# An overflow branch moved ahead of the last down block, splits held behind the norm, and the kernel's end in smaller parts

## The chip, the cores and the metric

The kernel runs on one core of a Trainium2 chip. The metric is the device time of one execution in microseconds, the median over runs of the same program. The core has five engines with queues of their own: TensorE (PE; its weight loads are listed as PEld), VectorE (DVE), ScalarE (ACT), GpSimd (POOL) and SyncE (SP), which only issues transfers here.

## The reference

Two blocks run one after the other on 256 tokens of width 1024. The first has two layers; each is a mixer (gated linear attention beside a gated spatial unit), a cross attention to 256 memory rows and a mixture of 16 experts, each followed by a layer norm. The second has one layer: a mixer (block attention beside a state-space scan), a mixture of 16 experts, and a gated addition before a last RMS norm. The parts that the change touches:

```
def grouped_moe(x, w_router, b_router, w_gate, w_up, w_down):
    ...
    for e in range(N_EXPERTS):
        h = jax.nn.silu(xt @ w_gate[e]) * (xt @ w_up[e])
        y = y + gate[:, e:e + 1] * (h @ w_down[e])
...
    x = layer_norm(DN_ALPHA * x + h, ln_g[l, 2], ln_b[l, 2])
...
# second_block, after hier_moe
    x = x + jax.nn.sigmoid(x @ w_ple_gate[i]) * (p[i] @ w_ple_proj[i])
return rms_norm(x, final_norm_g)
```

Each token uses two of the 16 experts. `hier_moe` in the second block computes the same sum over experts with another router.

## The kernel before

**Dense projections.** A float32 weight is loaded as pieces of up to 1 MB into `raw` buffers (`load`, line 156) and split into a high and a low part (`piece`, line 166, which calls `split`, line 221): ScalarE copies the high part to `whl`, VectorE subtracts it from the weight (lines 98 and 78 of the profile). Three matmuls make one product: high by high, high by low, low by high. There are six `whl` buffers of 2 x 512 columns.

**Experts.** `moe` (line 848) gathers up to 64 tokens for each expert and goes over the experts in eight pairs. For each pair come two up blocks (`up`, two times 16 matmuls a half), a product of both (`middle`), flips of it (`turned`), and the down block of the pair before (`down`, line 981). The evictions of a down block are a scaled copy on ScalarE (`dh` or, in the last pair, `dd`) and a scaled difference on VectorE (`dl`, `dd`), and `spread` (line 1002) brings them back to the tokens, adding into four PSUM tiles `Y` (`ysum`). The last pair has its down block and two spreads behind the loop. Expert weights are 96 transfers of 1 MB in a fixed order on SyncE's queue, into whatever buffers come free (`raw`, `whl`'s, `t8`'s and `vec`'s).

**Overflow.** Each expert has 64 places. If one was chosen by more tokens, a flag is set (line 1025), and `overflow` (line 1036) adds what is missing to `Y` in a loop over the experts, under a branch on every engine (flag load at line 1042, branch at line 1043). With these inputs the flag is not set. The branch is coded behind the last spread and behind `fill("next")`, which issues the loads of the next layer's first weights.

**What follows an expert layer.** In the first block `layer_norm` (line 280): residual sums of `x` with `Y`, mean and variance (in the second layer with a square on ScalarE), normalising, and `turn` (line 445), which flips `x` on TensorE (`trp`), applies gain and offset per column on ScalarE and VectorE alternately (`t`) and splits it (`xTh`, `xTl`). The products of `x` itself with gain and offset are put off to `flush` (line 502), which the next mixer calls behind its second projection in the first block and behind its first in the second block. Behind the first layer the value projection of the memory (`mem_v`, `acc<-whl,mTh`) is coded ahead of the norm. In the second block `tail` (line 1376) adds `Y`, turns `x`, projects it, and ends with the gated sum, the norm over 1024 columns (`rms_norm`, line 466) and one store per half of the tokens (line 1406).

**What sets the order.** A planner orders the instructions of each engine ahead of time by a simulated timeline and moves work over the branch where nothing forbids it. Instructions inside `urgent(name)` are preferred if the name is in `hp`; `after(ins)` queues what is traced inside it behind `ins` on that engine; matmuls of the expert layer and all loads on SyncE keep their written order.

Of the kernel before, what the change touches and what calls it, by code (L numbers as in the profile page):

```python
# [11 lines left out]
OP = mybir.AluOpType  # L12
# [11 lines left out]

class Net:
    def __init__(self, tc, aps, cap=CAP, fallback=True, layers=2, bufs=(7, 6, 9, 2), flex=(1, 2, 2), late=2,
                 hp=("ln", "xm"), ao=1, plat=7, an=((0, 4), (0, 5), 0)):
        self.hp = hp
        self.ao = ao
        self.plat = plat  # L30
        self.an = an
        self.late = late
        self.flex = flex
        self.early = {}
        self.ready = {}
        self.due = []
        self.bufs = bufs
        self.layers = layers
        self.tc, self.nc, self.a = tc, tc.nc, aps
        self.cap = cap  # L40
        self.fallback = fallback
# [124 lines left out]
    def piece(self, W, k0, segs, nk=4):  # L166

        key = W.tensor.name, W.offset, k0, segs[0][0]
        if key in self.ready:
            return self.ready.pop(key)  # L170
        raw = self.early.pop(key, None)
        if raw is None:
            raw = self.load(W, k0, segs, nk)
        n = raw.shape[-1]
        gr = self.GR if n <= 512 else 1
        out = []
        for j in range(0, nk, gr):
            hl = self.sb.tile([128, 2, gr, n], F32R, tag="hl", name="whl", bufs=self.NHL)
            self.split(hl[:, 0], hl[:, 1], raw[:, j:j + gr])
            out += [(hl[:, 0, i], hl[:, 1, i]) for i in range(gr)]  # L180
        return out

# [94 lines left out]
            self.nc.gpsimd.dma_start(v[:, i, :n], self.bcast(a, n))  # L277
        return v

    def layer_norm(self, x, l, i, at_once=False):  # L280


        nc = self.nc
        v = self.vec([self.a["ln_g"][l, i], self.a["ln_b"][l, i]])
        r = self.t8("xTh", [128, KT, T], F32R), self.t8("xTl", [128, KT, T], F32R)
        gb = self.cols[:, 0, i], self.cols[:, 1, i]

        tmp = {}

        def part(tt, c, A):  # L290
            with self.urgent("ln"):
                return steps(tt, c, A)

        def steps(tt, c, A):
            o = [x[:, tt, i * 512:(i + 1) * 512] for i in range(2)]
            if c == 0:
                tmp[tt] = self.sm("st", [128, 2, 6])
            st = tmp[tt]
            with self.after(tmp.get("first")):
                if at_once:  # L300
                    self.stt(o[c], o[c], ALPHA, A, OP.mult, OP.add, accum_out=st[:, 0, c:c + 1])
                else:
                    self.stt(o[c], o[c], ALPHA, A, OP.mult, OP.add)
                    nc.vector.bn_stats(st[:, c, :], o[c])
            if c == 0:
                return
            mv = self.sm("mv", [128, 2])
            rs = self.sm("rs", [128, 1])
            if at_once:
                self.ts(mv[:, 0:1], st[:, 0, 0:1], st[:, 0, 1:2], -1.0 / D, OP.add, OP.mult)  # L310
                tmp["first"] = self.ts(mv[:, 1:2], mv[:, 0:1], 0.03125, None, OP.mult).ins
                ss = self.sm("ss", [128, 1])
                self.act(r[1][:, :, tt * 128:(tt + 1) * 128], x[:, tt, :].rearrange("p (a b) -> p a b", a=KT), AF.Square,
                         scale=0.03125, bias=mv[:, 1:2], accum_out=ss)
                self.rsqrt(rs, ss, 1e-5, near=True)
            else:
                nc.vector.bn_aggr(mv, st)
                self.rsqrt(rs, mv[:, 1:2], 1e-5, near=True)
            for c in range(2):
                self.ts(o[c], o[c], mv[:, 0:1], rs, OP.add if at_once else OP.subtract, OP.mult)  # L320
                self.turn(r, x, tt, c, gb)

            def rest():
                self.mul(x[:, tt, :], x[:, tt, :], v[:, 0, :])
                self.add(x[:, tt, :], x[:, tt, :], v[:, 1, :])
            self.due.append(rest)
        return part, r
# [117 lines left out]
    def turn(self, r, x, tt, c, gb=None):  # L445

        p = self.rp([128, 4, 128], "trp")
        for j in range(4):
            kk = 4 * c + j
            last = self.nc.tensor.transpose(p[:, j, :], x[:, tt, kk * 128:(kk + 1) * 128], self.ident)  # L450
        o = [t[:, 4 * c:4 * c + 4, tt * 128:(tt + 1) * 128] for t in r]
        if gb:
            t = self.s2("t32", [128, 4, 128])
            for j in range(4):
                g, b = (v[:, 4 * c + j:4 * c + j + 1] for v in gb)
                if j % 2:
                    self.ts(t[:, j, :], p[:, j, :], g, b, OP.mult, OP.add)
                else:
                    self.act(t[:, j, :], p[:, j, :], AF.Identity, scale=g, bias=b)
            self.anchor = self.split(o[0], o[1], t).ins  # L460
        elif len(o) == 2:
            self.split(o[0], o[1], p)
        else:
            return last.ins, self.cp(o[0], p).ins
# [36 lines left out]

    def flush(self):

        for f in self.due:
            with self.tc.issue_after(self.anchor):
                f()
        self.due = []
# [340 lines left out]
    def moe(self, lg, xs, second, finish, gc, route, Wg, Wu, Wd, fill, source):  # L848
# [129 lines left out]
                    h = slice(64 * s, 64 * s + 64)  # L978
                    self.ts(DT[i][h], p[h, s], self.slot[h], None, OP.is_equal)

        def down(i, apart=False):

            h = H.pop(i)
            ps = [self.rp([128, 512], "dn") for _ in range(2)]
            ws = {(s, jh): self.expert(W, 2, 2 * i + s, jh) for jh in range(2) for s in range(2)}
            todo = [(f, c) for c in range(2) for f in range(4)] if apart else \
                [(f, c) for f in range(4) for c in range(2)]
            for f, c in todo:
                for s in range(2):
                    self.mmp(ps[c][64 * s:64 * s + 64], h[:, f, 64 * s:64 * s + 64],  # L990
                             ws[s, f // 2][:, f % 2, c * 512:(c + 1) * 512], f == 0, f == 3)
            PS[i] = []
            with self.urgent("dn"):
                room = self.t8("dd", [128, 2, 2, 512], F32R) if apart else None
                for c, p in enumerate(ps):
                    dh, dl = (room[:, c, 0], room[:, c, 1]) if apart else \
                        (self.s2(n, [128, 512], F32R) for n in ("dh", "dl"))
                    self.act(dh, p, AF.Copy, scale=gsl[:, i:i + 1])
                    self.stt(dl, p, gsl[:, i:i + 1], dh.bitcast(F32), OP.mult, OP.subtract)
                    PS[i].append((dh, dl))  # L1000
# [10 lines left out]
        for i in range(NE // 2):  # L1011
            pg = up(i, 0)
            if i > 1:
                spread(i - 2)
            gather(i // 2 * 4 + 4, (4 * (i % 2),))
            pu = up(i, 1)
            h = middle(pg, pu)
            if i:
                down(i - 1)
            gather(i // 2 * 4 + 4, (4 * (i % 2) + 2,))  # L1020
            if i == 0:
                slot_gates()
            if i == last and over:
                self.tc.keep_in_program_order(
                    nc.vector.tensor_scalar(flag, cm, float(self.cap), None, op0=OP.is_gt))
            rows(i)
            fill(i)
            turned(i, h)
        down(last, True)
        spread(last - 1)  # L1030
        spread(last)
        fill("next")
        self.overflow(over, Y, source, Wg, Wu, Wd)
        return Y

    def overflow(self, over, Y, source, Wg, Wu, Wd):
# [339 lines left out]
    def tail(self, x, Y, ple):  # L1376
# [3 lines left out]
        for tt in range(2):  # L1380
            for c in range(2):
                o = x[:, tt, c * 512:(c + 1) * 512]
                self.add(o, o, Y[tt, c])
                self.turn(xT, x, tt, c)
        out = self.t8("fin")

        def part(tt, c, A):
            g = self.s2("pg8", [128, 512])
            s = slice(c * 512, (c + 1) * 512)
            self.act(g, A, AF.Sigmoid)  # L1390
            self.mul(ple[:, tt, s], ple[:, tt, s], g)
            self.add(ple[:, tt, s], ple[:, tt, s], x[:, tt, s])
            if c:
                self.rms_norm(ple, None, out, v, (tt,))
        self.proj_full(xT, a["w_ple_gate_2"][0], part)
        return out

    def run(self, out, upto=None):
        tc = self.tc
        self.NRAW, self.NHL, self.NT8, self.GR = self.bufs  # L1400
        with tc.tile_pool(name="sb", bufs=1) as self.sb, \
                tc.tile_pool(name="ps", bufs=1, space=PSUM) as self.ps:
            r = self.body(upto)
            o = out[0].rearrange("(t p) d -> p t d", p=128)
            for tt in range(2):
                self.nc.sync.dma_start(o[:, tt, :], r[:, tt, :])

    def body(self, upto):
        nc, a = self.nc, self.a
# [7 lines left out]
        for l in range(self.layers):  # L1417
# [59 lines left out]
                    vs(0)  # L1477
            Y = self.moe(*got, gc, self.route1, a["w_gate"][l], a["w_up"][l], a["w_down"][l], fill, x)
            fill("tail")
            part, xT = self.layer_norm(x, l, 2, l + self.ao > 1)  # L1480
            for tt in range(2):
                for c in range(2):
                    part(tt, c, Y[tt, c])
# [60 lines left out]
```

## Time and profile before

| what | value |
|---|---|
| median of 3 runs | 1460.03 us (1458.52 to 3515.89) |
| profiled execution, own time | 1460.11 us |
| its span | 1458.3 us |
| mean granted clock of TensorE | 0.976 |
| TensorE matmuls busy | 94% of the span |
| VectorE, ScalarE busy | 44%, 35% |
| bytes read | 419.18 MB |

The span goes from the first to the last instruction. Busy shares are means over stages of different kinds: the three expert layers lie near 265 to 485, 705 to 926 and 1200 to 1420 us; the rest are projections, attention and scans. In a timeline row the columns are start, duration (of all merged instructions), engine, line, operation, output and inputs, shapes, count, and in brackets the idle time before and what ended it.

### The profile page before, as it was taken

How to read it: one execution, taken by the hardware profiler on the slowest of the kernel's cores; microseconds unless marked ns; L12 is line 12 of the kernel's file. 1: busy time of each engine (PE TensorE's matmuls, PEld its weight loads, DVE VectorE, ACT ScalarE, POOL GpSimd, SP SyncE). 2: the span in 40 equal slices, each digit the busy share in tenths (PEclk: the TensorE clock that was granted, in tenths of full speed). 3: DMA queues.
4: the chain of work that ended last, by engine and by line, in shares of the span. 5: the costliest groups of instructions: out<-in, count | busy, mean ns of one | idle time of the engine just before them, and what ended most of it. 6: DMA issues, size and time to landing. Idle time of an engine off the chain costs nothing. (4 is left out here: it accounts for less than half of the span.)

```text
span 1458.3 us, 18050 instructions
## 1 busy us (share of the span) xinstructions
PE 1375.7 (94%) x7258; PEld 899.7 (62%) x7258; DVE 636.3 (44%) x1088; ACT 504.8 (35%) x784; POOL 63.7 (4%) x107
## 2 busy tenths in 40 slices
PE   8999999999988898999899998799999979999987
PEld 7889897444433686898444433499878864444335
DVE  5754754412111767654512111657776641212134
ACT  5634443211101474443211101548764440111132
POOL 2110000000000103000000000000000000000000
PEclk9999999999999999999899999899999989999998
DMA  9745557799999965446799999844534679999991
GB/s 341 271 173 173 174 178 267 280 399 421 420 419 420 320 224 175 145 174 243 297 404 380 422 420 420 326 133 134 185 129 137 227 288 378 421 380 420 420 380 44
DMA packets 101964, 421.50 MB, mean 289 GB/s; under 512 B 10676, under 2 KB 10896, under 8 KB 65008
## 3 DMA queue, kind: packets, MB, share of 16 engines
q1 hardware_dynamic: 97968, 409.17, 72.4%
q0 software_dynamic: 3904, 11.09, 2.3%
q8 instruction: 60, 0.98, 0.3%
q14 instruction: 32, 0.26, 0.0%
HBM read 419.18 MB, written 1.05 MB: 288 GB/s over the span
## 5 line engine op out<-in xcount | busy, mean ns | idle before, releaser
L64 PE MATMUL gu<-we,XG 128*64 128x512 f32 x1536 | 347.0, 596 | 4.2 <-DMA we<-in_w_up_dram 1.9
L78 DVE TENSOR_TENSOR whl<-raw,whl 128x1024 fp32r<-128x1024 f32 (+1 forms) x210 | 241.1, 1163 | 144.6 <-ACT whl L98 143.7
L98 ACT ACTIVATE whl<-raw 128x1024 fp32r<-128x1024 f32 (+1 forms) x210 | 208.2, 1009 | 200.8 <-PE acc L64 97.2
L64 PEld LDWEIGHTS gu<-we,XG 128*64 128x64 f32 x1536 | 108.1, 137 | 208.2 <-issue 193.9
L64 PE MATMUL acc<-whl,xTh 128*128 128x512 f32 (+2 forms) x640 | 193.0, 387 | 4.6 <-ACT xTh L98 3.4
L64 PE MATMUL dn<-we,mid 128*64 128x512 f32 x768 | 179.3, 599 | 16.0 <-DMA we<-in_w_down_dram 13.9
L64 PEld LDWEIGHTS dn<-we,mid 128*64 128x64 f32 x768 | 58.0, 138 | 130.2 <-issue 101.6
L64 PEld LDWEIGHTS acc<-whl,xTh 128*128 128x128 f32 x640 | 119.6, 194 | 29.9 <-ACT xTh L98 4.0
L64 PE MATMUL facc<-xTh,whl 128*128 128x256 f32 x640 | 123.8, 289 | 1.7 <-ACT xTh L98 1.7
L64 PE MATMUL acc<-whl,xTl 128*128 128x512 f32 (+1 forms) x320 | 119.8, 385 | 0.2 <-DVE xTl L78 0.2
L95 ACT ACTIVATE dh<-dn,gsl 128x512 fp32r<-128x512 f32 x42 | 28.9, 688 | 258.8 <-PE dn L64 258.8
L78 DVE TENSOR_TENSOR mid<-mid,gu 128x512 f32<-128x512 f32 x24 | 25.3, 1056 | 211.3 <-PE gu L64 138.7
L64 PEld LDWEIGHTS facc<-xTh,whl 128*128 128x128 f32 x640 | 103.2, 195 | 2.4 <-ACT xTh L98 1.9
L64 PE MATMUL facc<-xTl,whl 128*128 128x256 f32 x320 | 91.6, 287 | 0.0
L87 DVE SCALAR_TENSOR_TENSOR dl<-dn,gsl,dh 128x512 fp32r<-128x512 f32 x42 | 31.5, 750 | 127.6 <-ACT dh L95 125.2
L95 ACT ACTIVATE XG<-gath,gc 128x256 f32<-128x256 f32 x48 | 25.3, 535 | 125.8 <-PE gath L64 117.8
L64 PEld LDWEIGHTS acc<-whl,xTl 128*128 128x128 f32 x320 | 60.5, 193 | 12.7 <-issue 0.7
L64 PEld LDWEIGHTS facc<-xTl,whl 128*128 128x128 f32 x320 | 61.9, 193 | 0.5 <-issue 0.3
L92 DVE TENSOR_SCALAR XG<-gath,gc 128x256 f32<-128x256 f32 x32 | 17.1, 543 | 100.6 <-ACT XG L95 100.2
L95 ACT ACTIVATE mid<-gu 128x512 f32<-128x512 f32 x24 | 14.3, 595 | 121.9 <-PE gu L64 115.4
L64 PE MATMUL acc<-whl,oTh 128*128 128x512 f32 x160 | 49.5, 402 | 0.5 <-ACT oTh L98 0.5
L64 PEld LDWEIGHTS gath<-Dm,xsh 128*128 128x128 f32 x192 | 30.7, 221 | 27.0 <-issue 17.1
(366 smaller groups left out, 1759.3 us busy)
## 6 DMA issues: line engine op xcount, KB each, us to landing
we<-in_w_gate_dram SPq DMA_DIRECT2D x96, 1024.0 KB, 12.7
we<-in_w_up_dram SPq DMA_DIRECT2D x96, 1024.0 KB, 11.8
we<-in_w_down_dram SPq DMA_DIRECT2D x96, 1024.0 KB, 16.7
raw<-in_w_in_dram SPq DMA_DIRECT2D x38, 1024.0 KB, 10.2
raw<-in_w_out_dram SPq DMA_DIRECT2D x12, 1024.0 KB, 5.0
raw<-in_wk_x_dram SPq DMA_DIRECT2D x8, 1024.0 KB, 9.1
raw<-in_wv_x_dram SPq DMA_DIRECT2D x8, 1024.0 KB, 5.7
raw<-in_wq_x_dram SPq DMA_DIRECT2D x8, 1024.0 KB, 5.0
```

The source lines that it names most:

```text
L64: return self.nc.tensor.matmul(out, lhsT=l, rhs=r, start=start, stop=stop, skip_group_check=True)
L78: return self.nc.vector.tensor_tensor(out, a, b, op=op)
L87: return self.nc.vector.scalar_tensor_tensor(out, a, s, b, op0=op0, op1=op1, **k)
L92: return self.nc.vector.tensor_scalar(out, a, s1, s2, op0=op0, op1=op1)
L95: return self.nc.scalar.activation(out, a, f, **k)
L98: return self.nc.scalar.activation(out, a, AF.Copy)
```

## The change

- `overflow` is called behind the eight pairs but ahead of the last down block. The last pair's down weights are requested ahead of it and handed to `down`; the flag is set one pair earlier. `fill("next")` stays behind the spreads and so comes behind the branch.
- `layer_norm` remembers, where `hold` is given (the last norm of each layer of the first block), the last normalising instruction on VectorE and ScalarE's last affine instruction in the turn of the last half of the tokens; until `flush`, splits of weights are queued behind these two.
- `"dn"` joins `hp`, so the evictions of all down blocks are preferred.
- In `tail` the sums of squares are taken per piece as it is made (512 columns, and two times 256 for the second half of the columns), the mean's scaling step moves from GpSimd to VectorE, and the final product and the stores are done in halves of 512 columns.

```diff
-                 hp=("ln", "xm"), ao=1, plat=7, an=((0, 4), (0, 5), 0)):
+                 hp=("ln", "xm", "dn"), ao=1, plat=7, an=((0, 4), (0, 5), 0)):
...
-            self.split(hl[:, 0], hl[:, 1], raw[:, j:j + gr])
+            with self.after(self.hold and self.hold[0]), self.after(self.hold and self.hold[1]):
+                self.split(hl[:, 0], hl[:, 1], raw[:, j:j + gr])
...
-                self.ts(o[c], o[c], mv[:, 0:1], rs, OP.add if at_once else OP.subtract, OP.mult)
-                self.turn(r, x, tt, c, gb)
+                n = self.ts(o[c], o[c], mv[:, 0:1], rs, OP.add if at_once else OP.subtract, OP.mult)
+                a = self.turn(r, x, tt, c, gb)
+            if tt and hold:
+                self.hold = n.ins, a
...
-                    self.act(t[:, j, :], p[:, j, :], AF.Identity, scale=g, bias=b)
+                    first = self.act(t[:, j, :], p[:, j, :], AF.Identity, scale=g, bias=b)
             self.anchor = self.split(o[0], o[1], t).ins
+            return first.ins
...
     def flush(self):
+        self.hold = None
...
-        def down(i, apart=False):
+        def down(i, apart=False, held=None):
...
-            ws = {(s, jh): self.expert(W, 2, 2 * i + s, jh) for jh in range(2) for s in range(2)}
+            ws = held or {(s, jh): self.expert(W, 2, 2 * i + s, jh) for jh in range(2) for s in range(2)}
...
-            if i == last and over:
+            if i == last - 1 and over:
...
-        down(last, True)
+        held = {(s, jh): self.expert(W, 2, 2 * last + s, jh) for jh in range(2) for s in range(2)}
+        self.overflow(over, Y, source, Wg, Wu, Wd)
+        down(last, True, held)
         spread(last - 1)
         spread(last)
         fill("next")
-        self.overflow(over, Y, source, Wg, Wu, Wd)
...
         def part(tt, c, A):
+            if c == 0:
+                ss[tt] = self.sm("ss4", [128, 4])
             g = self.s2("pg8", [128, 512])
-            s = slice(c * 512, (c + 1) * 512)
-            self.act(g, A, AF.Sigmoid)
-            self.mul(ple[:, tt, s], ple[:, tt, s], g)
-            self.add(ple[:, tt, s], ple[:, tt, s], x[:, tt, s])
+            for i, (c0, n) in enumerate(((0, 256), (256, 256)) if c else ((0, 512),)):
+                s, w = slice(c * 512 + c0, c * 512 + c0 + n), slice(c0, c0 + n)
+                self.act(g[:, w], A[:, w], AF.Sigmoid)
+                self.mul(ple[:, tt, s], ple[:, tt, s], g[:, w])
+                self.add(ple[:, tt, s], ple[:, tt, s], x[:, tt, s])
+                self.act(out[:, tt, s], ple[:, tt, s], AF.Square, scale=0.03125, accum_out=ss[tt][:, c + i:c + i + 1])
             if c:
-                self.rms_norm(ple, None, out, v, (tt,))
+                rs = self.sm("rs", [128, 1])
+                self.stt(rs, ss[tt][:, 0:1], ss[tt][:, 1:2], ss[tt][:, 2:3], OP.add, OP.add)
+                self.rsqrt(rs, rs, 1e-6, near=True)
+                for h in range(2):
+                    s = slice(h * 512, h * 512 + 512)
+                    self.stt(out[:, tt, s], ple[:, tt, s], rs, v[:, 0, s], OP.mult, OP.mult)
+                    self.nc.sync.dma_start(o[:, tt, s], out[:, tt, s])
...
-            part, xT = self.layer_norm(x, l, 2, l + self.ao > 1)
+            part, xT = self.layer_norm(x, l, 2, l + self.ao > 1, True)
```

## Rows read from the trace of the kernel before

**Rows 1.** The page: busy time of engines; costliest groups (busy, mean ns, idle before).

```profile
PE 1375.7 (94%) x7258; PEld 899.7 (62%) x7258; DVE 636.3 (44%) x1088; ACT 504.8 (35%) x784; POOL 63.7 (4%) x107
...
L95 ACT ACTIVATE dh<-dn,gsl 128x512 fp32r<-128x512 f32 x42 | 28.9, 688 | 258.8 <-PE dn L64 258.8
```

**Rows 2.** Timeline of PE, first junction (columns as told above).

```profile
486.81 0.73 PE L64 MATMUL acc<-whl,mTh 128*128 128x512 f32 x2 [0.87 <-DVE x L87]
...
502.81 0.39 PE L64 MATMUL acc<-whl,xTh 128*128 128x272 f32 x1 [2.79 <-ACT xTh L98]
```

**Rows 3.** Timeline of PE, second junction.

```profile
926.17 0.96 PE L64 MATMUL ysum<-dd,DT 128*128 128x512 f32 x3 [1.04 <-DVE dd L87]
933.06 3.67 PE L450 MATMUL trp<-ident,x 128*128 128x128 f32 x16 [5.92 <-DVE x L92]
937.35 1.22 PE L64 MATMUL acc<-whl,xTh 128*128 128x512 f32 x2 [0.62 <-ACT xTh L98]
```

**Rows 4.** Timeline of PE, third junction.

```profile
1420.25 0.96 PE L64 MATMUL ysum<-dd,DT 128*128 128x512 f32 x3 [0.91 <-DVE dd L87]
...
1426.60 1.64 PE L64 MATMUL acc<-whl,xTh 128*128 128x512 f32 x6
```

**Rows 5.** Stretches: length, busy (x instructions) of each engine, PEclk, DMA share, GB/s.

```profile
505.00:508.00 3.00, 3.00 (x15) 3.00 (x15) 3.00 (x4) 0.00 (x0) 0.00 (x0) 0.50 1.05 388
927.20:933.00 5.80, 0.00 (x0) 0.00 (x0) 5.04 (x17) 2.28 (x3) 0.56 (x1) 0.57 1.05 388
933.00:941.50 8.50, 7.82 (x26) 6.38 (x27) 7.41 (x17) 5.62 (x14) 0.55 (x1) 0.50 0.76 281
```

**Rows 6.** Timeline of ACT, second and third junction.

```profile
922.00 2.01 ACT L98 ACTIVATE whl<-raw 128x1024 fp32r<-128x1024 f32 x2 [0.76 <-PE dn L64]
923.91 0.67 ACT L95 ACTIVATE dd<-dn,gsl 128x512 fp32r<-128x512 f32 x1
...
1416.09 2.01 ACT L98 ACTIVATE whl<-raw 128x1024 fp32r<-128x1024 f32 x2 [0.73 <-DMA raw<-in_w_ple_gate_dram]
1418.00 0.67 ACT L95 ACTIVATE dd<-dn,gsl 128x512 fp32r<-128x512 f32 x1
```

**Rows 7.** Timeline of DVE, first and second junction.

```profile
505.20 4.62 DVE L78 TENSOR_TENSOR x<-x,vec 128x1024 f32<-128x1024 f32 x4
...
927.40 0.69 DVE L87 SCALAR_TENSOR_TENSOR x<-x,ysum 128x512 f32<-128x512 f32 x1 [0.15 <-DVEq L1043]
...
928.62 1.22 DVE L78 TENSOR_TENSOR whl<-raw,whl 128x1024 fp32r<-128x1024 f32 x1
```

**Rows 8.** Timelines of ACT and DVE at the end; the stores' landing.

```profile
1448.81 0.60 ACT L95 ACTIVATE pg<-acc 128x512 f32<-128x512 f32 x1 [1.75 <-PE acc L64]
1451.02 1.06 ACT L95 ACTIVATE fin<-ple 128x1024 f32<-128x1024 f32 x1 [1.62 <-DVE ple L78]
...
1453.11 1.28 DVE L87 SCALAR_TENSOR_TENSOR fin<-ple,rs,vec 128x1024 f32<-128x1024 f32 x1 [2.20 <-POOL rs L104]
...
DMA to landing us min/median/max: 2.6/2.6/2.6
```

**Rows 9.** Lines 1042, 1043: xcount, duration ns min/median/max, first and last start.

```profile
L1042 PEldq TENSOR_LOAD <-flag x3: 306/312/501, 483.6 to 1420.3; - x3
...
L1043 ACTq COMPARE_BRANCH  x3: 45/45/50, 482.8 to 1419.2; - x3
...
L1043 PEldq COMPARE_BRANCH  x3: 323/330/450, 484.3 to 1420.7; - x3
```

**Rows 10.** Timeline of PE at the first junction, last down block.

```profile
474.82 1.51 PE L64 MATMUL dn<-we,mid 128*64 128x512 f32 x6 [0.69 <-ACT mid L98]
```

**Rows 11.** SP: waits (total us, times, longest), third junction; a load at 496.

```profile
SPq L1043 <- SPq L1043: 14.1, 1, 14.1
...
L161 SPq DMA_DIRECT2D raw<-in_w_in_dram x1: 368/368/368, 496.1 to 496.1; - x1
...
DMA to landing us min/median/max: 5.2/5.2/5.2
```

More of the change, by code (lines that the diff above doesn't have):

```diff
@@ L278, in vec, with layer_norm @@
         return v
-    def layer_norm(self, x, l, i, at_once=False):
+    def layer_norm(self, x, l, i, at_once=False, hold=False):
         nc = self.nc
@@ L502, in flush @@
     def flush(self):
+        self.hold = None
         for f in self.due:
@@ L1385, in tail @@
         out = self.t8("fin")
+        o = self.out[0].rearrange("(t p) d -> p t d", p=128)
+        ss = {}
         def part(tt, c, A):
+            if c == 0:
+                ss[tt] = self.sm("ss4", [128, 4])
             g = self.s2("pg8", [128, 512])
-            s = slice(c * 512, (c + 1) * 512)
-            self.act(g, A, AF.Sigmoid)
-            self.mul(ple[:, tt, s], ple[:, tt, s], g)
-            self.add(ple[:, tt, s], ple[:, tt, s], x[:, tt, s])
-            if c:
-                self.rms_norm(ple, None, out, v, (tt,))
+            for i, (c0, n) in enumerate(((0, 256), (256, 256)) if c else ((0, 512),)):
[4 more added lines that the diff above has]
+                self.act(out[:, tt, s], ple[:, tt, s], AF.Square, scale=0.03125, accum_out=ss[tt][:, c + i:c + i + 1])
+            if c:
+                rs = self.sm("rs", [128, 1])
[5 more added lines that the diff above has]
+                    self.nc.sync.dma_start(o[:, tt, s], out[:, tt, s])
         self.proj_full(xT, a["w_ple_gate_2"][0], part)
@@ L1402, in run @@
                 tc.tile_pool(name="ps", bufs=1, space=PSUM) as self.ps:
[L1403 to L1406, printed above, removed]
+            self.out = out
+            self.body(upto)
     def body(self, upto):
```

## The prediction

> **What bounds the kernel now.** I read the page first, then the granted clock by stretch, then the timelines of single engines at the three places that the edits touch, and last the branch itself. TensorE is busy for 1375.7 us of the span [rows 1], so all its waiting is 82.6 us, and an edit that moves evictions, splits and a branch can give back only the part that lies at its own places: the three ends of an expert layer (near 485, 926 and 1420 us; I call them junctions) and the kernel's end. The reader is to see at each junction what TensorE waits for. At the first it waits 0.87 us behind the spread, then fills the norm with the next layer's value projection, and waits 2.79 us for the turned x [rows 2]. At the second there is nothing to fill with: it waits 1.04 us for the last eviction, 5.92 us for the norm and 0.62 us for the turned x [rows 3]. At the third it waits 0.91 us for the last eviction, and dense projection work starts only at 1426.60 [rows 4]. Around the first two the granted clock falls to 0.50, the lower level of 1.2 GHz: for 3.0 us at the first, and for nearly all of 8.5 us at the second, 7.8 of them busy, behind a stretch with no matmul at all [rows 5].
>
> Second reading: what stands in front of the late operation. At the second junction ScalarE runs two splits of the next weights (2.01 us) right before it evicts the last half of the down block at 923.91; at the third the same, 2.01 us before 1418.00 [rows 6]. VectorE puts a 1.22 us split between the pieces of the residual sum, 0.69 us each [rows 7]. So each part of the change has something to remove, but little of it.
>
> **The change part by part.** The sum stands against the profiled execution's own 1460.11 us (span 1458.3, the rest around it), which is the median of the runs shown (1460.03) but for 0.08.
>
> First junction (branch earlier, splits held, eviction first). What can go: 0.87 + 2.79 us of waiting, and half of the 3.0 us at clock 0.50, which is 1.5; together 5.2. What stays: the turn of x, its affine part on ScalarE and VectorE and its split must still follow the flips, unless the flips get in among the projection's matmuls. I take the first wait whole (0.9, x is read while the spread still runs), half of the second (1.4), half of the clock's part (0.7): 3.0. Bounds: 5.2, and below nothing, since the held splits move onto the path (under the rivals).
>
> Second junction. Eviction first: 1.0 gained. The residual sum of the first column no longer waits for a branch behind the spread: two pieces can lie beside the spread, about 0.6 us apart, 1.2, and the 1.22 us split leaves the norm's chain: 2.4 off the 5.92 us wait. Against it: the weights' first split, so far done ahead of the norm's end [rows 7], now follows the last normalised piece, one ScalarE split of 1.0 us and one VectorE split of 1.22, and is late next: −2.2. Of the four held splits only the first is on the path; the others run beside matmuls on the one before. I keep the clock's loss as it is (half of the 7.8 us, 3.9), since TensorE still idles through the norm. Sum 1.2. Bounds: −2.2, and 1.0 + 2.4 + half of 3.9, 5.3.
>
> Third junction (nothing is held there: the hold ends at the flush before). Eviction first 0.9, two pieces of x beside the spread 1.2: I take 2.1. Bounds: 4.1 (the 0.91 and half of the 6.35 us from 1420.25 to 1426.60, since flips and the split of x stay), and −1.3 (second rival).
>
> The kernel's end. After the last matmul the chain is sigmoid, two VectorE operations, a square over 1024 columns of 1.06 us, two GpSimd steps, a product of 1.28 us, and a store that lands 2.6 us after its issue [rows 8]. With halves, the first half's sigmoid, product and sum run beside the second's on the other engine, and the last square covers 256 columns: I count 0.5. The first GpSimd step becomes a short VectorE one (0.1), the product's second half replaces the whole (half of 1.28 is hidden behind the first store's issue, but the second still follows: 0.2), and the store is half as big: 0.4 of its 2.6. Sum 1.2; bounds 0 (shorter operations mostly pay their fixed part) and 2.5 (square, product and store all halved: 0.53 + 0.64 + 1.3). The added squares and issues for the earlier pieces lie beside TensorE's last matmuls.
>
> The branch before the last down block. On TensorE's sequencer it is a flag load of 0.31, a compare of 0.32 to 0.45 and one event [rows 9]. There TensorE already waits 0.69 us for the turned hidden units [rows 10], and sequencer work can run beside queued flips, so I charge 0.3 us at each of three branches, 0.9; bounds 0 and the whole 0.31 + 0.45 each, 2.3. The compare on ScalarE takes 0.05 [rows 9], and the rows show no engine standing still behind this branch with its inputs ready. The Trainium skill, "Runtime: NRT & Kernel Launch", section "Instruction fetch mechanics", speaks against this: a taken branch to a page that is not loaded stops the engine until the page has come. By that rule the upper bound of this term would hold and the time be 1454.9; by the rows it is 1453.5.
>
> Everything else at zero. The 42 evictions that gain priority already start when the matmuls end: ScalarE's wait before them is 258.8 us, all put down to TensorE [rows 1], and the expert loop is fed by weights in order. The flag is one small VectorE operation moved one pair earlier, beside the loop. SyncE's issue order up to the last down weights is the same.
>
> SyncE itself is the step whose price the trace hides. Behind its branch it executes eight event waits; at the third junction these take 14.1 us, until every transfer issued before has landed [rows 11]. Now this costs nothing, because the next weights are issued ahead of it. If they come behind it, the first goes out when the last down weights have landed, into an empty queue, where 1 MB takes 5.2 us from its issue [rows 11], in place of the 2.7 that 1.05 MB takes in a full one at 388 GB/s [rows 5]: 2.5 us late at each junction. At the second the held splits come later than that; at the first the first projection has the spread ahead of it. I take zero, as work coded behind the branch is already seen ahead of it (the splits at 1416.09 are coded behind it, and ScalarE's branch is at 1419.2 [rows 6, 9]); the price is in the second rival.
>
> Sum: 3.0 + 1.2 + 2.1 + 1.2 − 0.9 = 6.6, and 1460.1 − 6.6 = 1453.5.
>
> **The rivals.** First, slower: the hold only moves the wait. If the norm's chain gets no shorter, the first projection waits for splits that used to be ready. Its place is the first matmul on the new x at the first two junctions. Price: at the second 2.2; at the first half of that for 528 columns in place of 1024, 1.1, and, if the four operations on x (4.62 us) come between the norm and the low halves, 4.6 more [rows 7]. It decides when the part of these 7.9 us that comes exceeds what the rest gives (1.0 + 2.1 + 1.2 − 0.9 = 3.4); all of it makes 1460.1 + 7.9 − 3.4 = 1464.6. For it: VectorE has no free moment in the 3 us after the first new matmuls [rows 5]. Against: those operations are coded behind the first projection's splits.
>
> Second: SyncE's event waits stand in front of the next weights. ScalarE's order at the third junction puts a split of the second piece before the last eviction [rows 6]; weights 2.5 us later move that eviction from 1418.00 to 1420.5: its 0.9 becomes −2.5, and the 2.1 becomes −1.3. Time: 1453.5 + 3.4 = 1456.9.
>
> Third: the change does not do what it says. The compiler already carries work across the branch, so its place may not matter; then the overlap of x with the spread and the shorter norm are not new, and the two evictions and the end are left: 1.0 + 0.9 + 1.2 = 3.1, 1457.0.
>
> Fourth: everything fits and all bounds are reached, 5.2 + 5.3 + 4.1 + 2.5 = 17.1: 1443.0.
>
> **How the numbers follow.** Forecast (1450 to 1456.5) 0.45; first rival 0.18; second 0.12; third 0.13; fourth, from 1450 down, 0.12. The range 1445 to 1465 takes in the second and third rival and most of the first, and leaves out the far end of the fourth and the first rival's worst. A measurement of this kernel can tell about 2% (29 us) from no change; only a reshuffled schedule far from the junctions reaches that: faster 0.02, within 0.95, slower 0.03.
>
> **What would show it.** Right: no split of next weights between the last two evictions at 922; TensorE's wait before the flips of the second junction near 3.5 us instead of 5.92, with a new wait of 1 to 2 us for the first split; dense work of the third junction 2 us sooner after its last down matmul; from the last sigmoid's start to the end of the span 8.3 instead of 9.5 us [rows 8]. Wrong: a wait on the first split above 4 us at the first junction; next weights that land 2.5 us later and an eviction behind them; a gap of 1 us on TensorE between the hidden units' flips and the last down block.

## The result, and the profile after

The changed kernel takes 1467.65 us in the median of 9 runs (1466.09 to 1472.97), the kernel before 1460.88 in the 9 runs beside it (1456.47 to 1464.54, and one far off at 3515.89 that the ratio leaves out): ratio 1.0052, 95% interval 1.0038 to 1.0066, slower by half a per cent. The profiled execution took 1466.9 us, 6.8 more than before's, with a span of 1465.1 us.

I cut both traces into four stretches by landmarks on TensorE: **A** from the first matmul of the first layer's last down block to the first `po` (an output product) of the mixer behind it; **B** the same for the second layer; **C** from the third layer's first `plp` matmul (the product with `w_ple_proj`) to the first matmul of the last two spreads; **D** from there to the end of the span. First the landmarks of the kernel before that were not shown yet (A begins with [rows 10]), as rows of its PE timeline, then those of after with TensorE's waits:

```profile
566.61 0.62 PE L64 MATMUL po<-S,qT 128*64 128x256 f32 x2 [0.79 <-DVE S L611]
...
911.90 0.65 PE L64 MATMUL dn<-we,mid 128*64 128x512 f32 x2 [0.69 <-ACT mid L98]
...
988.40 0.77 PE L64 MATMUL po<-va,apT 128*128 128x64 f32 x5
...
1402.03 1.18 PE L64 MATMUL plp<-whl,pT 128*128 128x512 f32 x4
...
1416.07 0.50 PE L64 MATMUL ysum<-dh,DT 128*128 128x512 f32 x1
```

```profile
472.67 7.09 PE L65 MATMUL dn<-we,mid 128*64 128x512 f32 x32 [0.82 <-ACTq L1050]
484.61 0.73 PE L65 MATMUL acc<-whl,mTh 128*128 128x512 f32 x2 [0.76 <-DVE x L88]
...
501.19 0.59 PE L65 MATMUL acc<-whl,xTh 128*128 128x272 f32 x1 [3.37 <-ACT whl L99]
...
565.43 0.62 PE L65 MATMUL po<-S,qT 128*64 128x256 f32 x2 [0.79 <-DVE S L617]
...
911.85 0.65 PE L65 MATMUL dn<-we,mid 128*64 128x512 f32 x2 [0.73 <-ACTq L1050]
...
923.65 2.00 PE L65 MATMUL ysum<-dd,DT 128*128 128x512 f32 x8
929.18 3.81 PE L454 MATMUL trp<-ident,x 128*128 128x128 f32 x16 [3.52 <-DVE x L93]
936.01 0.80 PE L65 MATMUL acc<-whl,xTh 128*128 128x512 f32 x1 [3.02 <-ACT whl L99]
937.27 0.80 PE L65 MATMUL acc<-whl,xTh 128*128 128x512 f32 x1 [0.47 <-DVE whl L79]
...
988.06 0.88 PE L65 MATMUL po<-va,apT 128*128 128x64 f32 x6
...
1401.65 2.81 PE L65 MATMUL plp<-whl,pT 128*128 128x512 f32 x11
...
1413.67 1.94 PE L65 MATMUL dn<-we,mid 128*64 128x512 f32 x2 [5.73 <-DMA we<-in_w_down_dram]
1416.55 4.34 PE L65 MATMUL dn<-we,mid 128*64 128x512 f32 x8 [0.94 <-DMA we<-in_w_down_dram]
1422.27 5.36 PE L65 MATMUL dn<-we,mid 128*64 128x512 f32 x22 [1.38 <-SPq L1050]
1427.57 0.50 PE L65 MATMUL ysum<-dh,DT 128*128 128x512 f32 x1
```

The reader is to see two things. The first two junctions hardly moved: the wait for the flips at the second is 3.52 us in place of 5.92 [rows 3], but behind it stands a new one, 3.02 and 0.47 us for the first split of the weights. And in the third layer the last down block now waits for its own weights, 5.73 + 0.94 + 1.38 us (the last is put down to SyncE's branch, which has no work for TensorE; at that moment the last down weight lands); before it waited 0.74 us in all. The page says the same in one group: idle time before the down matmuls is 23.2 us, 20.2 of it for the DMA; before it was 16.0 and 13.9. SyncE's timeline says why, after first and then before:

```profile
1387.05 12.40 SPq L162 DMA_DIRECT2D raw<-in_w_ple_gate_dram  x4
1399.50 4.32 SPq L215 DMA_DIRECT2D we<-in_w_down_dram  x4
```

```profile
1385.56 16.50 SPq L213 DMA_DIRECT2D we<-in_w_down_dram  x4
1402.10 4.38 SPq L161 DMA_DIRECT2D raw<-in_w_ple_gate_dram  x4
```

The next weights (`w_ple_gate`, four transfers of 1 MB) have overtaken the last four down weights. These go out from 1399.50 to 1403.4 and land 14.0 to 18.8 us later, the last at 1422.2; in the kernel before the last down weight lands at 1410.6. Of C's 11.9 us more, 7.3 are waits; the rest is that the same matmuls take longer, ten of them at a mean granted clock of 0.66 between 1413.6 and 1422.2 us. What sets the end of C is the last landing: the last 22 matmuls start with it, at 1422.27. The PE rows above answer to [rows 2 to 4] and [rows 10]; those that answer to the other groups follow, one fence a view and with its columns: the page [rows 1], a stretch [rows 5], ScalarE [rows 6 and 8], VectorE [rows 7], the stores' landing [rows 8], the branch [rows 9] and SyncE's wait at the third junction [rows 11]:

```profile
PE 1379.8 (94%) x7258; PEld 898.7 (61%) x7258; DVE 637.0 (43%) x1098; ACT 504.4 (34%) x794; POOL 62.0 (4%) x105
...
L65 PE MATMUL dn<-we,mid 128*64 128x512 f32 x768 | 183.8, 604 | 23.2 <-DMA we<-in_w_down_dram 20.2
```

```profile
933.00:941.50 8.50, 5.03 (x11) 3.66 (x12) 8.14 (x12) 8.50 (x13) 0.00 (x0) 0.50 0.31 94
```

```profile
921.81 0.69 ACT L96 ACTIVATE dd<-dn,gsl 128x512 fp32r<-128x512 f32 x1 [2.75 <-PE dn L65]
...
934.89 5.79 ACT L99 ACTIVATE whl<-raw 128x1024 fp32r<-128x1024 f32 x6
940.57 1.16 ACT L99 ACTIVATE xTh<-t 128x512 fp32r<-128x512 f32 x2
...
1456.85 0.66 ACT L96 ACTIVATE pg<-acc 128x256 f32<-128x256 f32 x2 [2.20 <-PE acc L65]
```

```profile
924.32 0.69 DVE L88 SCALAR_TENSOR_TENSOR x<-x,ysum 128x512 f32<-128x512 f32 x1 [1.03 <-PE ysum L65]
```

```profile
DMA to landing us min/median/max: 2.0/2.0/2.1
```

```profile
L1050 PEldq COMPARE_BRANCH  x3: 318/318/353, 471.8 to 1405.5; - x3
L1050 ACTq COMPARE_BRANCH  x3: 45/45/50, 472.4 to 1408.3; - x3
```

```profile
SPq L1050 <- SPq L1050: 18.3, 1, 18.3
```

ScalarE evicts the second junction's last half at 921.81 in place of 923.91, idle for 2.75 us before it, and the residual sum starts at 924.32 in place of 927.40; but then it runs the six held splits in a row, 5.79 us, with half of x's high parts behind them. The end takes 1465.1 − 1456.85 = 8.3 us, and a half store lands in 2.0 us in place of 2.6.

All kernels of the study by the four stretches (us, from the landmark rows of each trace; the kernels are told below):

| kernel | A | B | C | D |
|---|---|---|---|---|
| before | 91.8 | 76.5 | 14.0 | 42.2 |
| after | 92.8 | 76.2 | 25.9 | 37.6 |
| e1 after, loads in order | 91.6 | 76.4 | 14.3 | 40.8 |
| e2 before, branch moved | 90.2 | 76.3 | 25.9 | 38.7 |
| e3 after, no hold | 90.5 | 76.1 | 26.0 | 37.6 |
| e4 before, hold | 92.7 | 78.1 | 14.0 | 42.4 |
| e5 before, four weights ahead | 91.3 | 76.6 | 24.8 | 39.6 |
| e6 before, two ahead | 91.3 | 76.6 | 21.1 | 39.6 |
| e7 e1, two splits free | 90.1 | 73.0 | 14.4 | 40.3 |
| e8 e1, no hold | 90.6 | 76.2 | 14.2 | 40.9 |
| e9 before, new end | 91.7 | 76.4 | 14.0 | 41.2 |
| e10 e7, branch at the old place | 91.1 | 74.3 | 14.3 | 41.0 |
| e11 e7, three free | 89.8 | 73.0 | 14.4 | 40.3 |
| e12 e7, no priority | 90.0 | 73.0 | 14.4 | 40.3 |

Before, e5, e6 and e9 have the same work in A and B: 91.3 to 91.8 and 76.4 to 76.6 is how well a stretch repeats. After and e1 differ in A by 1.2 with the same work, so A is good to about 1 us. One cause is in after's ScalarE timeline: two splits ahead of the last eviction at the first junction wait for a value weight, which e1's do not:

```profile
478.71 2.01 ACT L99 ACTIVATE whl<-raw 128x1024 fp32r<-128x1024 f32 x2 [1.66 <-DMA raw<-in_wv_x_dram]
```

After against before: +1.0, −0.3, +11.9, −4.6, in all +8.0; the span differs by 6.8. The rest lies outside the stretches: A begins 2.2 us earlier in that one execution, which e1 (1.5 us later there) doesn't repeat, and from A's end to B's start it takes 1.1 us longer.

### The profile page after: what moved, and what is told of

Same layout as the page of the kernel before. It is cut to its first block, busy times and chain, and to the rows that moved or that the text cites. A ratio compares the mean times of both kernels' runs of the same rounds, so it can differ in the third digit from the quotient of the medians.

```text
span 1465.1 us, 18082 instructions
## 1 busy us (share of the span) xinstructions
PE 1379.8 (94%) x7258; PEld 898.7 (61%) x7258; DVE 637.0 (43%) x1098; ACT 504.4 (34%) x794; POOL 62.0 (4%) x105
## 5 line engine op out<-in xcount | busy, mean ns | idle before, releaser
L65 PE MATMUL dn<-we,mid 128*64 128x512 f32 x768 | 183.8, 604 | 23.2 <-DMA we<-in_w_down_dram 20.2
L65 PEld LDWEIGHTS acc<-whl,xTl 128*128 128x128 f32 x320 | 60.7, 193 | 11.9 <-issue 0.3
L96 ACT ACTIVATE mid<-gu 128x512 f32<-128x512 f32 x24 | 14.3, 596 | 121.9 <-PE gu L65 109.0
```

The lines of the kernel that those rows point to most:

```text
L65: return self.nc.tensor.matmul(out, lhsT=l, rhs=r, start=start, stop=stop, skip_group_check=True)
L96: return self.nc.scalar.activation(out, a, f, **k)
```

## The experiments

**Theory:** the order of the loads in the third layer is the loss. **Rivals:** the held splits cost it; the branch ahead of the last down block stops TensorE.

**e1: only the request of the next weights goes back ahead of the branch.** Edit of the changed kernel:

```
         held = {...}
+        fill("next")
         self.overflow(over, Y, source, Wg, Wu, Wd)
...
         spread(last)
-        fill("next")
```

> The changed kernel with the next weights of all three layers requested between the request of the last down weights and the branch, in place of behind the spreads. Theory (in the third layer the next weights go ahead of the last four down weights on SyncE's queue, because the branch between the two requests removed the pin that kept their order; 4 MB of the queue, near 10 us): the four w_ple_gate loads are issued behind the last down weights again, the last spread of the third layer starts within 1.5 us of before's 1416.07 in place of 1427.57, and the time is 1457 to 1460 (the 6.8 us lost and the 1.2 us won at the end, less what the first two junctions change). Rival (the held splits and the earlier branch cost it, the order of the loads is covered by buffers): the time stays at 1464 or above.

1459.69 us against 1461.44; ratio 0.9987 (0.9971 to 1.0002). SyncE's and TensorE's timelines, third junction:

```profile
1387.89 16.50 SPq L215 DMA_DIRECT2D we<-in_w_down_dram  x4
1404.44 4.41 SPq L162 DMA_DIRECT2D raw<-in_w_ple_gate_dram  x4
```

```profile
1411.45 7.31 PE L65 MATMUL dn<-we,mid 128*64 128x512 f32 x32 [0.78 <-ACTq L1050]
1418.69 0.51 PE L65 MATMUL ysum<-dh,DT 128*128 128x512 f32 x1
...
1423.90 0.96 PE L65 MATMUL ysum<-dd,DT 128*128 128x512 f32 x3 [1.04 <-DVE dd L88]
```

The down weights are first again, C falls from 25.9 to 14.3 us, and the slowdown is gone; that e1 is faster than the kernel before is not shown. In the first two layers the loads go out as in the changed kernel, part of them behind the branch. The spread starts 2.6 us later than before's, over the 1.5 expected, but the whole trace was late by then (2.3 us at the first `plp`). The early branch itself costs 0.78 − 0.74 us of waiting.

**e2: the branch alone.** The kernel before with the branch, `held` and the flag as in the change:

```
+        held = {...}
+        self.overflow(over, Y, source, Wg, Wu, Wd)
+        down(last, True, held)
...
         fill("next")
-        self.overflow(over, Y, source, Wg, Wu, Wd)
```

> The kernel before with the branch moved, the last down weights requested ahead of it and the flag one pair earlier; no held splits, no eviction priority, the old end. Theory (order of the loads): the third layer's last spread starts near 1427 as in the changed kernel, and the time is 1466 to 1470, above the changed kernel by what its end wins. Rival (the hold costs it): 1459 to 1462.

1468.55 against 1461.44; 1.0045 (1.0032 to 1.0058). C is 25.9 as in the changed kernel, without a held split.

**e5 and e6: only the order of the loads.** The kernel before; in the third layer the tiles of the last down weights are taken first, their transfers issued behind four (e5) or two (e6) of the next weights:

```
+            held = {...}           # tiles only
+            fill("next0")          # two transfers of w_ple_gate
+            fill("next1")          # two more, e5 only
+            for g in go: g()       # the four down transfers
```

> The kernel before with one thing changed: in the third layer the four transfers of the next weights (w_ple_gate, 1 MB each) are issued ahead of the last four down weights, into the same buffers as before; branch, splits, evictions and end as before. Theory (the order of these loads is the whole loss): the last down block waits for its weights as in the changed kernel, the last spread of the third layer starts near 1427 us in place of 1416.07, and the time is 1466 to 1470. Rival (the branch ahead of the last down block holds TensorE, which the profile of the changed kernel hides under the wait for weights): at most 1462.

> As the kernel with four next weights ahead of the last down weights, but with two of them ahead and two behind. Theory (the queue delivers 1 MB in 2.7 us, in order): the last down weight lands 5.4 us later than before, at 1416, the last 22 matmuls of 5.4 us follow it, so that the last spread starts near 1422 in place of 1416.07 and 1427.57, and the time is 1462.5 to 1465.5. Rival (only the change of order matters, or buffers that come free late, whatever the bytes): as with four, 1466 to 1470, or as before, 1460 to 1462.

e5: 1467.65 against 1461.94; 1.0038 (1.0024 to 1.0052), C 24.8. e6: 1466.11, 0.6 above the range expected; 1.0030 (1.0016 to 1.0043), C 21.1. TensorE's timelines, e5 and then e6:

```profile
1416.86 1.94 PE L65 MATMUL dn<-we,mid 128*64 128x512 f32 x2 [5.99 <-DMA we<-in_w_down_dram]
1419.17 3.89 PE L65 MATMUL dn<-we,mid 128*64 128x512 f32 x8 [0.37 <-DMA we<-in_w_down_dram]
1424.11 5.36 PE L65 MATMUL dn<-we,mid 128*64 128x512 f32 x22 [1.05 <-SPq L1061]
```

```profile
1418.18 7.06 PE L65 MATMUL dn<-we,mid 128*64 128x512 f32 x22 [1.46 <-DMA we<-in_w_down_dram]
```

With the branch at its old place the order alone makes the waits and all but 1.1 us of C's loss; the rival with the branch falls. Two megabytes cost 7.1 us in C and four 10.8. e6's C is 1.2 us above the 5.9 expected: its last 22 matmuls took 7.06 us in place of 5.36, at a mean granted clock of 0.76 between 1418.2 and 1425.2 us, where before's ran at 1.00. Without these 1.7 us the two megabytes cost 5.4, as much for each as the four.

**e3, e8 and e4: the price of the hold.** e3 is the changed kernel, e8 is e1, each with `hold` not given; e4 is the kernel before with the hold alone:

```
-            part, xT = self.layer_norm(x, l, 2, l + self.ao > 1, True)
+            part, xT = self.layer_norm(x, l, 2, l + self.ao > 1)
```

> The changed kernel without the hold of the weights' splits. Theory (order of the loads): 1465 to 1469, because at the second junction the 2.4 us that the norm wins by the hold come back as the new wait of 3.0 us for the first split, and the third junction is untouched. Rival (the hold costs it, up to its two new waits of 3.4 and 3.0 us): 1460 to 1462.

> The changed kernel with the next weights requested ahead of the branch and no split held. Theory (the hold gives back what it takes): within 1.5 us of the kernel with the hold and the loads' order mended, 1458 to 1461. Rival (the hold costs 2 to 3 us): 1456 to 1457.5.

> The kernel before with the hold of the weights' splits alone; the branch, the priority and the end as before. Theory (order of the loads is the loss, the hold takes about what it gives): 1459 to 1462, with a new wait of 2 to 4 us for the first split behind each of the first two norms and a shorter wait for the flips. Rival (the hold costs it): 1463 to 1467.

e3: 1467.17 against 1461.44, 1.0031 (1.0018 to 1.0044). e8: 1458.88 against 1461.94, 0.9979 (0.9967 to 0.9991). e4: 1464.21 against 1461.44, 1.0016 (1.0003 to 1.0029). With the branch moved, B is 76.1 and 76.2 without the hold, 76.2 and 76.4 with it: it gives back what it takes. In A it costs 1.0 us (e1 against e8); the 2.3 of after against e3 have the wait of 1.66 us for the value weight in them. My expectation for e4 was wrong: on the old branch the hold costs 1.6 us in B and 0.9 in A. e4's VectorE shows why the norm gains less there:

```profile
926.19 0.69 DVE L88 SCALAR_TENSOR_TENSOR x<-x,ysum 128x512 f32<-128x512 f32 x1 [2.52 <-PEq L1049]
```

The first residual sum waits 2.52 us behind TensorE's branch, so that the flips wait 4.77 us in place of the changed kernel's 3.52, while TensorE waits for the first split about as long as there (2.99 and 0.77 us). With the branch at its old place the full hold takes more than it gives.

**e7: two splits free.** e1, but the first two splits behind each norm aren't held:

```
+            hold = self.hold if self.free <= 0 else None
+            self.free -= 1
-            with self.after(self.hold and self.hold[0]), ...
+            with self.after(hold and hold[0]), ...
...
                 self.hold = n.ins, a
+                self.free = 2
```

> The changed kernel with the next weights requested ahead of the branch, and with the first two splits behind each norm not held. Theory (the hold gives the norm 2.4 us at the second junction and takes 3.0 back because the very first split waits too; ScalarE stands idle for 2.75 us ahead of the last eviction, where two splits fit): the wait of 3.0 us for the first split at the second junction is gone or below 1 us, the flips there stay early, and the time is 1.5 to 4 us under the kernel with the order of loads mended, 1455.5 to 1458.5. Rival (what is held does not matter, the norm's chain was covered anyway): within 1 us of it, 1459 to 1461.

1454.80 against 1461.94, 0.7 under the range expected; 0.9949 (0.9930 to 0.9967): the fastest of the study with e11 and e12 below, under both kernels. Second junction, ACT and PE:

```profile
917.48 2.00 ACT L100 ACTIVATE whl<-raw 128x1024 fp32r<-128x1024 f32 x2
920.19 0.69 ACT L97 ACTIVATE dd<-dn,gsl 128x512 fp32r<-128x512 f32 x1 [0.70 <-PE dn L66]
```

```profile
927.57 3.81 PE L458 MATMUL trp<-ident,x 128*128 128x128 f32 x16 [3.52 <-DVE x L94]
931.89 1.22 PE L66 MATMUL acc<-whl,xTh 128*128 128x512 f32 x2 [0.51 <-ACT xTh L100]
```

Two splits fit into ScalarE's idle time and leave the eviction waiting for TensorE alone. The flips stay early (3.52) and the wait behind them falls from 3.02 to 0.51. B is 73.0, 3.5 us under before's.

**e10 and e11: is the branch needed, and does a third split help?** e10 is e7 with the branch as before; e11 has `self.free = 3`.

> The kernel with two free splits behind each norm, but with the branch behind the last spread, as before. Theory (the hold pays only with the branch out of the way: VectorE's first residual sum waits 2.5 us behind TensorE's branch at the second junction when it is at the old place): the wait for the flips at the second junction is near 4.8 us in place of 3.5, and the time 1 to 3 us above the kernel with two free splits and the branch moved. Rival (the branch's place does not matter): within 0.7 us of it, with a wait near 3.5.

> As the kernel with two free splits and the branch moved, but with three free splits. Theory (ScalarE's free room ahead of the norm holds two splits, and a third lies between the last eviction and the norm's square, on no path until the square's input is there): within 1 us of it at the second junction, the wait for the flips between 3.5 and 4.7 us. Rival (any split that is done early shortens the path): another 1 us faster.

Against 1461.01: e10 1457.94, 0.9974 (0.9963 to 0.9984); e11 1455.03, 0.9961 (0.9947 to 0.9974). e10's wait for the flips is 4.77 us and B 74.3: the branch's place is worth 1.3 us in B once the splits are out of the way, and about 1 in A, which is no more than A repeats to. The third free split changes nothing that these runs can tell.

**e12: e7 without the priority of the evictions** (`"dn"` taken out of `hp`).

> As the kernel with two free splits and the branch moved, but without the priority of the down blocks' evictions. Theory (the priority changes no engine's order, so this is a second measurement of the same order): 5 to 9 us under the kernel before, as the first one (7.1). Rival (the priority brought the evictions forward, 1.0 us each at two junctions): 2 us above the first, with the wait of 1.03 us between the last two matmul groups of the second junction's spread.

1455.57; 0.9963 (0.9949 to 0.9976), with all four stretches as e7's. The instructions of every engine stand in the same order in e7 and e12, and in e2 and e3, which differ by `"dn"` and the new end, they do up to the end. On the kernel before, `"dn"` alone was not run.

**e9: the new end alone.**

```
-                self.rms_norm(ple, None, out, v, (tt,))
+                ...
+                for h in range(2):
+                    self.stt(out[:, tt, s], ...)
+                    self.nc.sync.dma_start(o[:, tt, s], out[:, tt, s])
```

> The kernel before with the new end alone (squares per piece, product and stores in halves). The forecast's term: 1.2 us faster, with 8.3 us in place of 9.5 from the start of the last sigmoid of its half to the end of the span. Rival (shorter operations and more stores only pay more fixed parts): within 0.4 us, near 9.5 us at the end.

1459.38 against 1461.01, 1.6 us; 0.9988 (0.9979 to 0.9998). D falls by 1.0 us, and from the last sigmoid (1450.89) to the end (1459.2) it is 8.3 us.

## Why the prediction was wrong

**The step that failed** is the sentence "SyncE's issue order up to the last down weights is the same", under "Everything else at zero". I read the branch as work on each engine and never asked what it parts. In the kernel before, the requests of the last down weights and of the next weights stand on one side of the branch, and loads there keep their written order; in the change a branch lies between them. What I wrote ahead of it, that all loads on SyncE keep their written order and that the next weights come behind the branch, does not hold across a branch: in the third layer the planner put the next weights ahead of the branch and of the last down weights. I had even noted that work coded behind the branch is seen ahead of it, and used that only to price SyncE's waits at zero. That the place of the request decides is shown by e1, that the order alone makes the loss by e5, the size by e5 and e6. How the planner weighs it, and why the first two layers keep the old order, was not tried and stays open. In before, the last down weights wait 5.8 us on SyncE for buffers that an earlier down block still holds, room that loads for other buffers can use; that fits, and no more.

The size: in e2, where the end is the old one, C grows by 11.9 us and D falls by 3.5. D's part is no gain of the kind that I had forecast for the third junction but a by-product of the wait: ScalarE does the splits during it. TensorE's waits of 0.91, 1.19 and 0.48 us behind the spread in before [rows 4, and the two below] shrink to one of 0.69, and the granted clock, 0.72 between 1421.3 and 1425.1 us in before, stays at 1.00 there:

```profile
1422.41 0.63 PE L450 MATMUL trp<-ident,x 128*128 128x128 f32 x4 [1.19 <-DVE x L78]
1423.51 1.97 PE L450 MATMUL trp<-ident,x 128*128 128x128 f32 x8 [0.48 <-DVE x L78]
```

Net 8.4; the new end takes 1.0 off it, and the profiled runs differ by 6.8.

**First junction, 3.0 forecast.** By A the changed kernel lost 1.0 and e1 won 0.2. The branch alone wins 1.2 to 1.6 (e8, e2), of which the wait of 0.87 us behind the spread is a part: it is gone in e1, e2, e3 and e8, though 0.76 of it stands in after's trace. The hold takes that back: the second wait, of which I had taken half away, is 3.37 us for a split where it was 2.79 for the turned x [rows 2], and the granted clock still falls there (0.57 between 501 and 505 us). That is the first rival's mechanism, at the size of a wait below the 4 us that I had named as its sign.

**Second junction, 1.2 forecast.** B won 0.3, 0.1 in e1. Eviction (2.1 us earlier) and flips (3.52, forecast 3.5) came as told; the new wait was 3.5 us, forecast 1 to 2. I had counted one split on each engine behind the last normalised piece; but the hold is set behind ScalarE's last affine instruction too, as the change says. In the trace the last normalised piece is ready at 931.75, and ScalarE starts the first split only at 934.89, VectorE at 935.99. The clock stays at 0.50 through this stretch, as I had assumed.

**Third junction, 2.1 forecast.** With the order mended (e1) C + D is 55.1 us, and 55.2 with only the new end (e9): 0.1 us. The eviction does not come sooner there: a wait of 1.04 us for it stands in e1, and one of 0.60 us ahead of it. My upper bound was also read wrongly: in before, flips already run from 1422.41 and the first two projection matmuls at 1425.13, not only from 1426.60. That the evictions gain by `"dn"` was wrong at this junction and the second: in e3 the second still has a wait of 1.03 us for the eviction, and after has none because the hold took the splits away. So the 1.0 us that I counted there for the priority came, but from the hold.

**The end, 1.2 forecast:** 1.0 by D in e9, 8.3 us from the last sigmoid as told.

**The branch on TensorE, −0.9 forecast:** 0.82 − 0.69, 0.73 − 0.69 and, in e1, 0.78 − 0.74: 0.2 in all. The Trainium skill's rule that I weighed there ("Runtime: NRT & Kernel Launch", section "Instruction fetch mechanics": a taken branch to a page that isn't loaded stops the engine) would have made it 2.3; these three waits show no such stop. Whether the branch's target was loaded by then, no trace here shows.

**The second rival, SyncE's event waits,** did not show. SyncE stands 9.6 us behind the first branch and issues the rest of the next weights only from 484.8, but no wait of TensorE in A is for them, and e8, with that branch and 8.5 us of event waits behind it, wins 1.2 there. The sign that I had named, an eviction behind late weights, is in after's trace (the 1.66 us for the value weight), but those loads were issued by 461.2, ahead of SyncE's branch at 474.53.

## What to carry to other kernels

Before a branch or another block border is moved, list for every queue what is requested on each side of it: a written order may hold only inside a block, and on a queue that was full here, four transfers in the wrong place cost about their whole time. A hold that clears an engine for an urgent chain should leave what fits into that engine's idle time in front of the chain; look at the first operation that is held, not at the sum. A priority that changes no engine's order is no part of a change, so compare the orders before it is priced.

## What the runs showed that was not expected

**The transfers finished in order of issue, at the queue's pace.** In before the last four down weights land at 1403.2, 1405.6, 1408.1 and 1410.6 us and the four next weights from 1413.3 to 1421.3; in e5 the next weights land from 1406.1 to 1414.1 and the down weights behind them, the last at 1424.1. e5 moved 4 MB ahead and C grew by 10.8 us, 2.7 a MB. The Trainium skill, "DMA: Bandwidth & Descriptors", section "Queues, rings and completion order", says that each DMA engine consumes its descriptors in ring order though completions may pass each other; these transfers of 1 MB agree with the first and show nothing of the second.

**The same order of instructions gets another clock from run to run.** e7 and e12 have the same instructions in the same order, but behind the same short waits, near 1087 us, the granted clock in e7's profiled execution falls to 0.50 (1.2 GHz) for about 7 us, and in e12's it stays at 1.00. Stretches of e7 and then e12:

```profile
1087.00:1090.00 3.00, 2.96 (x10) 2.67 (x11) 2.22 (x7) 0.70 (x2) 0.00 (x0) 0.50 0.92 341
1090.00:1093.00 3.00, 3.00 (x8) 2.32 (x8) 0.00 (x0) 0.00 (x0) 0.00 (x0) 0.50 0.01 2
```

```profile
1087.00:1090.00 3.00, 2.88 (x16) 2.48 (x17) 2.30 (x8) 0.78 (x2) 0.00 (x0) 1.00 0.92 337
1090.00:1093.00 3.00, 3.00 (x23) 2.74 (x21) 0.88 (x3) 1.04 (x4) 0.00 (x0) 1.00 0.04 12
```

e7's span is 3.0 us longer than e12's (1454.5 against 1451.5), and all of it arises between here and the third expert layer. The Trainium skill, "TensorE: Matmul & The Clock Gate", section "Part 1: The HAM clock gate (the "warmup" mystery)", says of a kernel's start that the number of slow matmuls varies from run to run; here it varies in the middle too. The same stretch, from B's end to C's start, takes 413.4 to 413.6 us in the eight profiles without such a fall, 416.5 to 416.6 in the four with one of this length (e3, e7, e8, e9), 415.2 in e10 with half of it and 417.9 in e4 with one and a half. But for the one far off, runs of the kernel before spread from 1456.47 to 1468.71 us over the study, so a term of one or two microseconds is read from stretches, not from a single time.
